# Spreading sixty-four multiply-adds on VectorE over sixteen gate products instead of nine

## The chip, the cores and the metric

One NeuronCore of a Trainium2 chip runs the whole program. The metric is the time of one execution on the device in microseconds (us), taken as the median of several executions; a profiled execution gives the rows quoted here.

## The reference, cut to what matters

The program is a two-layer backbone over 512 latent tokens and 256 context tokens with 2048 features. Layer 0 is an attention mixer, layer 1 a Fourier mixer. For this change, layer 1 matters:

```python
m = silu(cvec) @ ada_w + ada_b            # shift, scale, gate: 3 x 2048
h = layer_norm(x) * (1.0 + scale) + shift
u, gate = split(h @ w_in)                 # 4096 columns each
f = fft2(u in groups of 256).real         # over tokens and group
o = (f * silu(gate)) @ w_out
x = layer_norm(ALPHA * x + g_l * o) * ln_g + ln_b
```

The vector `m` of layer 1 has 6144 values, twelve chunks of 512. The chunks 0 to 7 (shift and scale) are needed before layer 1 starts. The chunks 8 to 11 (the gate `g_l`) are needed only when layer 1's output is scaled, long after the gate products. These four chunks are what the change moves.

## The kernel before, in words

**Where we are.** The Fourier layer runs in `fourier` (L1254 on): `transforms` makes the operands, `gates` computes the gate path in sixteen products g = 0 to 15 and stores silu of each, `mix` computes sixteen products for the other half and multiplies, then two output stages follow. `gates` takes the stretch from about 1218 to 1577 us.

**One gate product.** `product_pair` (L1194 on) forms one [256 x 2048] by [2048 x 512] product from seven smaller ones (i = 0 to 6), by combining 2 x 2 blocks. Each of the seven splits a weight block in two parts (high on ScalarE at L41 into `wh`, low on VectorE at L44 into `wl`), then TensorE multiplies 24 pairs of 128 x 128 by 128 x 256 (L54). The seven use the operands `ba`, `bb`, `bt` (four of them) and `bc`, and then the next gate begins with `ba` again. VectorE also adds block sums for the next product (L1183, L1184, L1185), changes one sum (L1206) and combines results from PSUM (L1212 to L1221, tile `c`). ScalarE applies silu (L1354, tile `sgo`), and its queue stores the result. `wh` and `wl` have three buffers each. So a split can start when the product three places back has ended.

**What is called between the products.** After product i the function `mid(i)` is called. `ahead` (L1228 on) acts at i = 4: it puts four weight loads of 512 KB each (`wraw`) on SyncE's queue and the three block sums for the next gate on VectorE. The weight loads go round five buffers, so they wait for the splits and sums that read the old blocks. In the gates 0 to 7 a further step at i = 6 loads a block of `hf` on SyncE's queue, forms four combinations on GpSimd (L1160 to L1165) and stores them from GpSimd's queue (`ht`).

**The conditioning chunks.** `mac_start` (L229) makes a generator, `tick` (L234) advances it by one step, `mac_rest` (L238) runs what is left. One step (`ada_steps`, L184 on) takes one tile `macraw` of [128, 2, 512] (512 KB), and does two multiply-adds of 128 x 512 on VectorE (L195 for the first of a chunk, L197 for the others) into a tile `mac`; then it issues the load of the next `macraw`. Four chunks of eight steps make 32 steps, 64 multiply-adds and 32 loads. When a chunk is full, the next tick calls `ada_col` (L215 on): four small matmuls of `mac` with a column of ones on TensorE into the PSUM tile `psm` (L219), then a small add on VectorE (L223) into `g1`.

**What sets the order.** From here to the end `pinned` is true, and every matmul stays in program order on TensorE. The loads of SyncE's queue are issued with `late`, so they stay in program order too. The multiply-adds, splits and sums on VectorE aren't held (`mac_hold` is False): the framework chooses their place in VectorE's instruction order at build time, and the engine then works strictly in that order.

**Before the change** `tick` is called at i = 0, 2, 4 and 6 of the gates 0 to 8. That is four steps and eight multiply-adds a gate. The 32 steps end with gate 7 and the last `ada_col` comes in gate 8. The gates 9 to 15 have none. `macraw` and `mac` have three buffers each at the right side of SBUF, freed after gate 8; there the five buffers of `stage` follow, which hold operands for the first product of `mix` (`spread` at L1245 splits them while gate 15 still runs).

Of the kernel before, what the change touches and what calls it, by code (L numbers as in the profile page):

```python
# [10 lines left out]
F32 = mybir.dt.float32  # L11
# [4 lines left out]
PSUM = bass.MemoryType.PSUM  # L16
# [8 lines left out]
class Build:  # L25
# [1314 lines left out]
    def gates(self, f, pair, ops):  # L1340
        nc = self.nc
        st = f.enter_context(ExitStack())
        sp = self.pool(st, "sgp", 1)
        with ExitStack() as m:
            macp = self.pool(m, "mac5", 3, side="right")
            tp = self.pool(m, "tmp5", 3, side="right")
            psm = self.pool(m, "psm5", 1, space=PSUM)
            self.mac_start(macp, lambda: tp.tile([128, 512], F32, name="mac"), lambda: psm.tile([128, 512], F32, name="psm5"),
                           [(1, 8), (1, 9), (1, 10), (1, 11)], 2)

            def gate(g, mid=self.ahead):
                c = pair(ops, mid)
                v = sp.tile([128, 4, 256], F32, name="sgo")
                nc.scalar.activation(out=v, in_=c, func=AF.Silu)  # L1354
                self.nc.scalar.dma_start(out=self.sg_d[g], in_=v)

            for g in range(9):
                def mid(i, g=g):
                    if i % 2 == 0:
                        self.tick()  # L1360
                    self.ahead(i)
                    if g < 8 and i == 6:
                        hf = tp.tile([128, 8, 256], F32, name="hf5", bufs=1)
                        self.load(hf[:, 4:8, :].rearrange("p a b -> p (a b)"), self.hf_d[g].rearrange("p a b -> p (a b)"), True)
                        self.combo_terms(hf[:, 6, :], hf[:, 7, :], hf[:, 4, :], hf[:, 5, :], hf[:, 0:4, :])
                        self.store(self.ht_d[:, :, g, :], hf[:, 0:7, :])
                gate(g, mid)
            self.mac_rest()
        self.fu = f.enter_context(ExitStack())
        self.stage_pool(self.fu, 5, self.ht_d)  # L1370
        for g in range(9, 16):
            gate(g)
            if g == 11:
                self.stage(5)
        st.close()

    def mix(self, f, pair, ops):
# [324 lines left out]
```

## Time and profile before

| | |
|---|---|
| median of 3 runs | 2333.34 us (2333.04 to 2336.59) |
| profiled execution, its own time | 2323.94 us |
| its span, first to last instruction | 2322.2 us |
| mean granted TensorE clock | 0.976 of full speed |
| TensorE matmul busy | 2147.6 us, 92% |
| VectorE busy | 1886.4 us, 81% |
| ScalarE busy | 947.0 us, 41% |
| GpSimd busy | 429.0 us, 18% |

Rows speak of PE (TensorE), DVE (VectorE), ACT (ScalarE), POOL (GpSimd) and SP (SyncE); a "q" behind the name is the engine's queue, which issues transfers. The profiled execution is 9.4 us below the median of the runs, so a saving read from its rows is subtracted from the median.

### The profile page before, as it was taken

The numbers are of one execution on the slowest core, as the hardware profiler recorded it, in microseconds if no ns is written. First come the engines' busy times: TensorE is split into PE (matmuls) and PEld (weight loads), VectorE is DVE, ScalarE is ACT, GpSimd is POOL, SyncE is SP. The second block draws the span as 40 slices with busy tenths as digits, with TensorE's granted clock in tenths as the row PEclk, the third lists the DMA queues.
The fourth block names the chain that finished last, engine by engine and source line by source line (L and its number), as shares of the span: only waits on it lengthen the run. The fifth ranks groups of instructions, "written<-read, shape, count | busy, mean of one in ns | idle before, by whom it ended". The sixth has DMA issues, their size and how long they took to land.

```text
span 2322.2 us, 39267 instructions
## 1 busy us (share of the span) xinstructions
PE 2147.6 (92%) x15708; PEld 1994.3 (86%) x15708; DVE 1886.4 (81%) x2603; ACT 947.0 (41%) x1321; POOL 429.0 (18%) x407
## 2 busy tenths in 40 slices
PE   5999989989999999999788999998999998998994
PEld 3778879889899999777568989998999998998994
DVE  5456799998765588677799998789899899779998
ACT  2222344433444467322463333444343445445331
POOL 1023413100111123000551131002122124002003
PEclk9999999999999999999999999999999999999997
DMA  8852354566511132787427765545455446537333
GB/s 339 310 196 95 124 183 159 188 230 208 208 48 58 60 110 75 229 300 261 169 96 252 273 242 181 182 146 188 156 175 193 150 166 230 174 128 255 117 137 118
DMA packets 128702, 412.63 MB, mean 178 GB/s; under 512 B 14852, under 2 KB 15492, under 8 KB 126728
## 3 DMA queue, kind: packets, MB, share of 16 engines
q1 hardware_dynamic: 113144, 359.04, 45.3%
q0 software_dynamic: 8320, 31.33, 3.8%
q10 hardware_dynamic: 7056, 19.76, 2.2%
q8 instruction: 123, 2.02, 0.4%
q14 instruction: 59, 0.48, 0.1%
HBM read 347.81 MB, written 62.26 MB: 177 GB/s over the span
## 4 chain that ended last, share of the span: by engine, by line
PE 35%; DVE 8%; DMA 3%; issue 3%; ACT 1%; POOL 1%; DVEq 0%; SPq 0%; ACTq 0%; POOLq 0%
PE r L54 33%; DVE wl L44 2%; DMA wraw<-in_wg 2%; PE psd L54 1%; DVE mac L197 1%; DMA stage<-yt 1%; DVE wraw L1185 1%; DVE btl L44 1%; DVE ws L1206 0%; DVE x L1539 0%; DVE c L1219 0%; PE pt L1492 0%; DVE hf L1325 0%; DVE x L1535 0%; POOL btl L44 0%
## 5 line engine op out<-in xcount | busy, mean ns | idle before, releaser
L54 PE MATMUL r<-bth,wl 128*128 128x256 f32 x1848 | 525.1, 284 | 16.8 <-DVE wl L44 16.5
L54 PE MATMUL r<-btl,wh 128*128 128x256 f32 x1848 | 524.6, 284 | 2.3 <-DVE btl L44 1.3
L54 PE MATMUL r<-bth,wh 128*128 128x256 f32 x1848 | 525.2, 284 | 0.2 <-ACT wh L41 0.2
L41 ACT CAST wh<-wraw 128x1024 fp32r<-128x1024 f32 x262 | 274.6, 1050 | 393.1 <-PE r L54 288.0
L44 DVE TENSOR_TENSOR wl<-wraw,wh 128x1024 fp32r<-128x1024 f32 x262 | 335.0, 1283 | 52.3 <-ACT wh L41 52.0
L54 PEld LDWEIGHTS r<-bth,wl 128*128 128x128 f32 x1848 | 351.4, 190 | 19.5 <-DVE wl L44 19.2
L54 PEld LDWEIGHTS r<-btl,wh 128*128 128x128 f32 x1848 | 350.8, 190 | 3.6 <-DVE btl L44 1.7
L54 PEld LDWEIGHTS r<-bth,wh 128*128 128x128 f32 x1848 | 351.8, 190 | 0.9 <-issue 0.5
L41 ACT CAST wh<-ws 128x1024 fp32r<-128x1024 f32 x183 | 191.8, 1049 | 344.3 <-PE r L54 330.4
L44 DVE TENSOR_TENSOR wl<-ws,wh 128x1024 fp32r<-128x1024 f32 x183 | 230.0, 1257 | 12.0 <-ACT wh L41 9.8
L197 DVE SCALAR_TENSOR_TENSOR mac<-macraw,cs,mac 128x512 f32<-128x512 f32 x240 | 193.6, 807 | 11.4 <-DMA macraw<-in_ada 9.9
L54 PE MATMUL r<-hlh,wl 128*128 128x256 f32 (+1 forms) x480 | 147.2, 307 | 26.7 <-DVE wl L44 26.6
L54 PE MATMUL r<-hlh,wh 128*128 128x256 f32 (+1 forms) x480 | 146.3, 305 | 0.6 <-ACT wh L41 0.5
L54 PE MATMUL r<-hll,wh 128*128 128x256 f32 (+1 forms) x480 | 144.9, 302 | 0.0
L54 PE MATMUL r<-bah,wl 128*128 128x256 f32 x384 | 112.7, 293 | 25.1 <-DVE wl L44 25.1
L54 PEld LDWEIGHTS r<-hlh,wl 128*128 128x128 f32 x480 | 93.5, 195 | 33.7 <-DVE wl L44 30.7
L41 ACT CAST pgh<-raw 128x512 fp32r<-128x512 f32 (+2 forms) x104 | 65.7, 662 | 121.8 <-DMA raw<-in_wo 78.2
L54 PE MATMUL r<-bbh,wl 128*128 128x256 f32 x384 | 109.5, 285 | 2.9 <-DVE wl L44 2.9
L54 PE MATMUL r<-bal,wh 128*128 128x256 f32 x384 | 111.2, 290 | 0.0
L54 PE MATMUL oacc<-pgl,yh 128*128 128x512 f32 x256 | 102.1, 399 | 9.7 <-DVE pgl L44 9.7
L54 PE MATMUL r<-bah,wh 128*128 128x256 f32 x384 | 111.1, 289 | 0.0
L54 PE MATMUL r<-bbh,wh 128*128 128x256 f32 x384 | 109.4, 285 | 0.0
(489 smaller groups left out, 5700.1 us busy)
## 6 DMA issues: line engine op xcount, KB each, us to landing
macraw<-in_ada SPq DMA_DIRECT2D x72, 512.0 KB, 6.3
wraw<-in_win SPq DMA_DIRECT2D x66, 512.0 KB, 6.7
raw<-in_adas SPq DMA_DIRECT2D x64, 512.0 KB, 5.1
wraw<-in_wg SPq DMA_DIRECT2D x64, 512.0 KB, 6.6
wraw<-in_wu SPq DMA_DIRECT2D x64, 512.0 KB, 4.3
wraw<-in_wo SPq DMA_DIRECT2D x64, 512.0 KB, 4.7
macraw<-in_ada SPq DMA_DIRECT2D x112, 256.0 KB, 3.9
raw<-in_wo SPq DMA_DIRECT2D x40, 512.0 KB, 5.4
```

Source lines behind the costliest of these rows:

```text
L41: ins = nc.scalar.copy(out=hi, in_=src)
L44: sub = (eng or nc.vector).tensor_sub(out=lo, in0=src, in1=hi.bitcast(F32))
L54: self.pin(self.nc.tensor.matmul(ps, lhsT=a, rhs=b, start=start, stop=stop))
L197: ins = nc.vector.scalar_tensor_tensor(out=acc, in0=raw[:, k, :], scalar=col, in1=acc, op0=ALU.mult, op1=ALU.add)
L1185: nc.vector.tensor_sub(out=raw[1, 0], in0=raw[0, 0], in1=raw[1, 0])
```

## The change

The pools of the conditioning work move out of the inner scope and live through the stage on the left side, with two buffers for `macraw` (three before) and two for `mac` (three before). `hf` alone stays on the right side. `tick` is called at i = 1 and 5 instead of 0, 2, 4, 6, and in all sixteen gates instead of nine. So a gate has two steps and four multiply-adds. `ada_col` falls in the gates 4, 8 and 12 (it was in 2, 4, 6 and 8), and the last one after gate 15, in `mac_rest`.

```diff
         st = f.enter_context(ExitStack())
         sp = self.pool(st, "sgp", 1)
+        macp = self.pool(st, "mac5", 2)
+        mp = self.pool(st, "acc5", 2)
+        psm = self.pool(st, "psm5", 1, space=PSUM)
+        self.mac_start(macp, lambda: mp.tile([128, 512], F32, name="mac"), lambda: psm.tile([128, 512], F32, name="psm5"),
+                       [(1, 8), (1, 9), (1, 10), (1, 11)], 2)
         with ExitStack() as m:
-            macp = self.pool(m, "mac5", 3, side="right")
-            tp = self.pool(m, "tmp5", 3, side="right")
-            psm = self.pool(m, "psm5", 1, space=PSUM)
-            self.mac_start(macp, lambda: tp.tile([128, 512], F32, name="mac"), lambda: psm.tile([128, 512], F32, name="psm5"),
-                           [(1, 8), (1, 9), (1, 10), (1, 11)], 2)
+            tp = self.pool(m, "tmp5", 1, side="right")
...
             for g in range(9):
                 def mid(i, g=g):
-                    if i % 2 == 0:
+                    if i in (1, 5):
                         self.tick()
                     self.ahead(i)
...
                 gate(g, mid)
-            self.mac_rest()
         self.fu = f.enter_context(ExitStack())
         self.stage_pool(self.fu, 5, self.ht_d)
         for g in range(9, 16):
-            gate(g)
+            def mid(i):
+                if i in (1, 5):
+                    self.tick()
+                self.ahead(i)
+            gate(g, mid)
             if g == 11:
                 self.stage(5)
+        self.mac_rest()
         st.close()
```

## Rows read from the trace of the kernel before

**Rows 1.** The page's first part: busy time, share of the span, instructions.
```profile
PE 2147.6 (92%) x15708; PEld 1994.3 (86%) x15708; DVE 1886.4 (81%) x2603; ACT 947.0 (41%) x1321; POOL 429.0 (18%) x407
```

**Rows 2.** Busy time by stretch, one gate each; then PE clock, DMA share, GB/s.
```profile
1217.80:1246.86 29.06, 22.70 (x169) 21.86 (x168) 27.86 (x33) 11.93 (x12) 5.26 (x6) 0.94 0.66 219
1246.86:1270.92 24.06, 21.12 (x172) 20.91 (x173) 22.82 (x28) 8.68 (x9) 6.26 (x6) 0.99 0.75 271
1270.92:1295.17 24.25, 23.07 (x182) 22.87 (x182) 22.09 (x27) 8.68 (x10) 5.58 (x5) 0.94 0.75 259
...
1388.67:1413.01 24.34, 20.47 (x167) 19.85 (x166) 21.92 (x26) 8.68 (x10) 7.29 (x7) 1.00 0.66 238
1413.01:1434.02 21.01, 21.01 (x178) 21.01 (x177) 16.73 (x19) 8.59 (x9) 0.00 (x0) 1.00 0.57 189
1434.02:1454.18 20.16, 20.16 (x170) 20.16 (x169) 15.74 (x17) 8.58 (x10) 0.00 (x0) 1.00 0.39 131
...
1554.98:1576.01 21.03, 21.03 (x178) 21.03 (x177) 19.82 (x21) 15.06 (x17) 1.71 (x1) 1.00 0.45 144
```

**Rows 3.** Waits of PE, from 1215 to 1425 us, then from 1425 to 1640.
```profile
PE r L54 <- DVE wl L44: 21.8, 12, 3.5
...
PE r L54 <- DVE wl L44: 9.5, 4, 4.0
```

**Rows 4.** Groups on DVE, 1246.86 to 1413.01 us (gates 1 to 7).
```profile
L197 DVE SCALAR_TENSOR_TENSOR mac<-macraw,cs,mac 128x512 f32<-128x512 f32 x53 | 44.3, 836 | 0.0
L44 DVE TENSOR_TENSOR wl<-wraw,wh 128x1024 fp32r<-128x1024 f32 x30 | 40.1, 1347 | 0.4 <-ACT wh L41 0.4
...
L1183 DVE TENSOR_TENSOR ws<-wraw 128x1024 f32<-128x1024 f32 x7 | 8.6, 1223 | 9.5 <-DMA wraw<-in_wg 9.5
...
L223 DVE TENSOR_TENSOR g<-psm,adab 128x4 f32<-128x4 f32 x3 | 0.5, 158 | 3.2 <-PE psm L219 3.2
```

**Rows 5.** Groups on DVE, 1434.02 to 1554.98 us (gates 9 to 14).
```profile
L44 DVE TENSOR_TENSOR wl<-wraw,wh 128x1024 fp32r<-128x1024 f32 x24 | 29.4, 1226 | 13.7 <-ACT wh L41 13.7
...
L1221 DVE TENSOR_TENSOR c<-r,c 128x256 f32<-128x256 f32 x6 | 2.5, 425 | 4.2 <-PE r L54 4.2
```

**Rows 6.** Timeline of DVE at the end of gate 1: start, duration, instruction.
```profile
1265.43 1.23 DVE L197 SCALAR_TENSOR_TENSOR mac<-macraw,cs,mac 128x512 f32<-128x512 f32 x1
...
1268.42 1.74 DVE L44 TENSOR_TENSOR wl<-wraw,wh 128x1024 fp32r<-128x1024 f32 x1
```

**Rows 7.** Timeline of PE at the start of gate 2.
```profile
1270.21 0.42 PE L54 MATMUL r<-bah,wl 128*128 128x256 f32 x1 [2.31 <-DVE wl L44]
...
1274.44 0.95 PE L219 MATMUL psm<-ones,mac 128*128 128x1 f32 x8
```

**Rows 8.** SP: its waits in gates 1 to 7, its timeline in gate 1; then the chain.
```profile
SPq L62 <- DVE mac L197: 65.4, 15, 10.7
...
1250.35 4.64 SPq L62 DMA_DIRECT2D wraw<-in_wg  x4
...
1252.91 7.53 DMA wraw<-in_wg
```

**Rows 9.** Timeline of DVE in gate 14, then of PE there.
```profile
1544.81 1.22 DVE L1183 TENSOR_TENSOR ws<-wraw 128x1024 f32<-128x1024 f32 x1
...
1547.41 1.22 DVE L44 TENSOR_TENSOR wl<-ws,wh 128x1024 fp32r<-128x1024 f32 x1
...
1550.02 1.22 DVE L44 TENSOR_TENSOR wl<-wraw,wh 128x1024 fp32r<-128x1024 f32 x1
...
1551.03 0.28 PE L54 MATMUL r<-bch,wh 128*128 128x256 f32 x1
...
1553.91 0.28 PE L54 MATMUL r<-bah,wh 128*128 128x256 f32 x1
```

**Rows 10.** Timeline of DVE from gate 15 into the first product of the mix.
```profile
1558.34 1.23 DVE L44 TENSOR_TENSOR wl<-wraw,wh 128x1024 fp32r<-128x1024 f32 x1 [0.74 <-ACT wh L41]
...
1612.32 1.23 DVE L44 TENSOR_TENSOR wl<-wraw,wh 128x1024 fp32r<-128x1024 f32 x1 [1.81 <-ACT wh L41]
```

## The prediction, made before the changed kernel was run

> **What bounds the kernel now.** I read the page first, then the busy time gate by gate, the waits, the groups of VectorE in the two halves of the stage, the timelines, and the queue of SyncE. Over the span TensorE's matmuls are busy 92% [rows 1], so time can be won only where TensorE stands. The gate table shows where [rows 2]. A row runs from one gate's silu to the next. From gate 9 on a gate takes 20.16 us with TensorE busy through all of it, while VectorE works 15.74 us. The gates 1 to 7 take 166.15 us together (1246.86 to 1413.01), 23.74 a gate, with VectorE busy 21.69 us on the mean of the seven rows (first 22.82, last 21.92). So in the first half VectorE alone needs more than TensorE's 20.16. TensorE's waits there are all for `wl`, the low part of a split weight: 21.8 us in 12 waits, the longest 3.5 [rows 3]. The multiply-adds of the conditioning chunks are VectorE's largest group in this stretch [rows 4]; they are absent from gate 9 on.
>
> One stall shows the mechanism. At the end of gate 1 a multiply-add of step i = 6 runs at 1265.43, the split of gate 2's first weight ends only at 1270.16 [rows 6], and TensorE starts at 1270.21 after 2.31 us of waiting [rows 7]. The matmul behind it took 0.42 us where it takes 0.28 in gate 14 [rows 7, 9], and the mean granted clock of that gate is 0.94 [rows 2]: for a few us the clock is at 1.2 instead of 2.4 GHz. That costs 24.25 x 0.06 = 1.5 us more.
>
> VectorE also stands still in gates 1 to 7: 9.5 us at the block sum L1183 for the landing of a weight, 3.2 us at the small add L223 for TensorE [rows 4]. The weight is late since SyncE's queue is in order: it waited 65.4 us for multiply-adds to free `macraw` buffers. In gate 1 it could issue the four weight loads only from 1250.35; one landed 7.53 us after 1252.91 [rows 8].
>
> **The change, part by part.**
>
> *Price of a multiply-add.* Eight of them and all that disturbs them make 21.69 - 15.74 = 5.95 us of VectorE in a gate: 0.74 each [rows 2]. Four fewer give back 2.98.
>
> *Gates 1 to 7.* VectorE needs 15.74 + 2.98 = 18.7 us, or 19.2 if disturbance by GpSimd, which doesn't go, is priced by itself: the splits of raw blocks take 1347 ns against 1226 from gate 9 on, 30 of them in seven gates, 0.5 us a gate [rows 4, 5]. Both are under 20.16, so TensorE becomes the bound. Lower end: 20.16 a gate. Upper end: VectorE keeps all its idle time of 23.74 - 21.69 = 2.05, so 19.2 + 2.05 = 21.25 a gate. I take the lower end and 3 us of leftover stalls over the seven, since the weights also come earlier (below). One `ada_col` remains here (gate 4) where there were three; gate 8, which had one and nothing else, took 21.01, so it costs 0.85 [rows 2]; the matmuls alone are 0.95 [rows 7]. Sum: 7 x 20.16 + 0.85 + 3 = 145.0. **Gain 21.2** (16.5 to 24.2).
>
> *Gate 0.* It takes 29.06 us with VectorE busy 27.86 [rows 2]. It holds eight multiply-adds; four go, 3.0 us. Its first wait, for the first split after the transforms, stays. **Gain 2.5** (0 to 4).
>
> *Gate 8.* It had no multiply-adds and gets four, but VectorE's 16.73 + 2.98 stays under 20.16, and `ada_col` is in it before and after. **0.**
>
> *Gates 9 to 15.* Four multiply-adds each, 2.98 us, go into VectorE's idle time of 20.16 - 15.74 = 4.42 us. That idle time is waiting for `wh` and for TensorE [rows 5], and lies in the first half of a gate, where the pair of i = 1 falls. The pair of i = 5 falls into the full half. There a split is ready early: in gate 14 the last split ends at 1548.63 and is used at 1551.03, the next gate's first ends at 1551.24 and is used at 1553.91 [rows 9]. The cover is 2.40 us, the pair takes 1.48. If both pairs fell there, 0.6 us a gate would show; nothing can be gained. **Loss 0.5** (0 to 4). `ada_col` in gate 12 adds **0.85**; TensorE, all busy there, can't hide it.
>
> *Into the mix.* From 1558.34 VectorE works with hardly a break until 1610.5 (the wait of 1.81 us before 1612.32) [rows 10], since the splits of `stage` join in. TensorE has its 9.5 us of waits of the second half here [rows 3]. What gate 15's four multiply-adds (2.98 us) can't put into gaps like the 0.74 us before 1558.34 moves everything behind them: **loss 2.0** (0.7 to 3.0). The last `ada_col`, 0.85, stands before mix's first product, partly where TensorE waits anyhow: **loss 0.4** (0 to 0.85).
>
> *The queues.* SyncE still issues 32 loads of 512 KB, now one ahead of each gate's four weight loads and one behind them, where three stood ahead and one behind. With two buffers the load for step n + 1 waits for the multiply-adds of step n - 1. The one ahead of the weights waits for those of i = 5 of the gate before; in gate 1 the last pair ran before gate 2's first matmul [rows 6, 7], so the weights are released near a gate's start, earlier than now. Behind it wait the weights, then L1183 and the splits; I price no delay, and its failure is a rival. The `hf` load and GpSimd's work stay behind the gate's last `macraw` load as before. `macraw` and `mac` stand at the left from gate 0 on, and `stage` takes the place of `hf` at the right; no wait comes of that, as far as I see. The DMA share in gate 9 is 0.39 [rows 2], so sixteen more loads find room. On GpSimd's and ScalarE's queues nothing is added. At the start the first `macraw` load comes one product later; nothing but the first pair waits for it. These go at zero.
>
> *Sum.* 21.2 + 2.5 - 0.5 - 0.85 - 2.0 - 0.4 = 19.95, say **20 us**. The profiled execution has 2323.94 us, so it would be 2304; the median of the runs is 9.4 us higher, and the forecast is 2333.34 - 20 = **2313**.
>
> *A rule against it.* GpSimd's combinations keep running in the gates 0 to 7, and VectorE's instructions are longer beside them: a multiply-add took 1.23 us and a split 1.74 [rows 6], against means of 0.84 and 1.35 [rows 4]. Over a gate the splits show the 0.5 us found above. The Trainium skill, SBUF — State Buffer, section "Who interferes with whom", says that a VectorE instruction with two SBUF inputs and a GpSimd instruction that reads SBUF hold the shared port in turn, and that the later one is blocked wholly. By that alone the sum would be about zero in gates 1 to 7; it is the second rival. The trace disagrees in the amount.
>
> **The rivals.**
>
> 1. *The stall follows the multiply-adds, not VectorE's fullness.* The gates 1 to 7 lose 23.74 - 20.16 - 3 x 0.85 / 7 = 3.2 us with eight, so 0.4 us each. Four in every gate then cost 1.6. Gates 1 to 7 gain 166.15 - 141.1 - 11.2 - 0.85 = 13.0, gate 0 gains 1.6, gate 8 loses 1.6, the gates 9 to 15 lose 11.2 + 0.85, the mix 2.4: a loss of 1.5, **2335**. For it: VectorE's order is chosen by the framework. Against it: 4.42 us idle and 2.40 us of cover [rows 2, 9].
>
> 2. *GpSimd blocks VectorE wholly.* GpSimd is busy 5.58 us in gate 2 [rows 2]. Then VectorE needs 18.7 + 5.6 = 24.3 us, as long as a gate takes now, and gates 1 to 7 gain nothing: 2.5 - 0.5 - 0.85 - 2.0 - 0.4 = a loss of 1.25, **2335**. Against it: with eight multiply-adds it would be 27.3, and a gate took 23.74.
>
> 3. *The ring of two holds back the weights* (the slower side). The block sum L1183 runs at 1544.81, 11.1 us after gate 14's first matmul (1553.91 - 20.16) [rows 9]. With a landing of 7.53 us [rows 8] its loads must be out some 3 us into a gate. If the i = 5 pair of the gate before ends later than that, L1183 blocks VectorE's order, and the 0.9 us of cover left after the pair is gone. With 1 us of stall and 1.5 of lowered clock a gate takes 22.7: gates 1 to 7 gain 166.15 - 158.6 - 0.85 = 6.7, gate 8 loses 2.5, the gates 9 to 15 lose 17.5 + 0.85, the mix 2.4: a loss of 16.6, **2350**. For it: SyncE's 65.4 us of such waits [rows 8]. Against it: in gate 1 the i = 6 pair was over before 1268.42, about when gate 2 could have begun (1270.21 - 2.31), some 3 us ahead of that point, with twice the multiply-adds in front of it.
>
> **How the numbers follow.** The forecast has 0.86, rival 1 0.05, rival 2 0.03, rival 3 0.06. Best case of the terms: 24.2 + 4 - 0.85 - 0.7 = 26.6, 2307; worst: 16.5 - 4 - 0.85 - 3.0 - 0.85 = 7.8, 2326. VectorE's order elsewhere may shift by a few us too, so I give 2304 to 2326; under 2 in 10 are left out, the rivals and the tails. A measurement of this kernel can tell 0.2%, 4.7 us, from no change. Faster 0.86 (the forecast), same 0.08 (rivals 1 and 2), slower 0.06.
>
> **What would show it.** Right: gates 1 to 7 near 20.2 to 21 us with VectorE near 19, clock 1.00, TensorE's waits for `wl` from 21.8 down to a few us, no wait of L1183 for a weight; gates 9 to 14 still 20.16 with VectorE near 18.7 (gate 12 21.0); the mix starting with some 2 us more VectorE work. Wrong: waits of a few us per gate in the second half (rival 1), GpSimd's combinations with long VectorE instructions beside them and gates near 24 us (rival 2), L1183 waiting for weights behind `macraw` loads in all gates (rival 3).

## The result, and the profile after

The changed kernel took 2304.53 us (median of 4, 2301.56 to 2308.92), the kernel before, run beside it on the same chip, 2333.19 us. The ratio is 0.9884 (95% interval 0.9868 to 0.9900), so the change saves 1.2%, 23 to 31 us. The forecast was 2313 us, a saving of 20, with a range of 2304 to 2326. The measured time is 8.5 us below the forecast and half a us inside the fast end of the range.

The two profiled executions differ by less: 2323.94 and 2301.56 us, 22.4 us. The reason lies ahead of the stage. Up to the first gate matmul both programs have the same instructions in the same order on every engine, but this matmul comes at 1217.42 us before and at 1221.96 after. In the fourteen profiled executions of this study it lies between 1217.4 and 1228.0. So a stretch is compared from its own first instruction, not from the start of the program. From the first gate matmul to the first result of the mix (`yt`) it is 397.84 us before and 371.00 after: 26.8 us. Behind that the two agree to 0.1 us (706.90 and 706.83).

| stretch (us) | before | after | gain | forecast |
|---|---|---|---|---|
| first matmul to silu of gate 0 | 29.44 | 27.20 | 2.2 | 2.5 |
| gates 1 to 7 | 166.15 | 142.22 | 23.9 | 21.2 |
| gate 8 | 21.01 | 19.44 | 1.6 | 0 |
| gates 9 to 15 | 141.99 | 142.01 | 0.0 | -1.35 |
| silu of gate 15 to the first `yt` | 39.25 | 40.13 | -0.9 | -2.4 |
| sum | 397.84 | 371.00 | 26.8 | 20.0 |

The busy time by gate of the changed kernel answers to [rows 2], in the same columns: bounds and length, then PE, PEld, DVE, ACT, POOL, clock, DMA share, GB/s. Its first row begins with the first gate matmul.

```profile
1221.96:1249.16 27.20, 24.52 (x190) 24.28 (x189) 27.07 (x33) 12.04 (x12) 4.46 (x4) 0.94 0.72 231
1249.16:1268.19 19.03, 19.03 (x161) 19.03 (x160) 18.93 (x22) 8.58 (x10) 7.37 (x6) 1.00 0.79 272
1268.19:1290.35 22.16, 22.16 (x187) 22.16 (x186) 20.82 (x23) 8.68 (x10) 7.29 (x8) 1.00 0.70 238
...
1370.39:1391.38 20.99, 20.99 (x177) 20.99 (x177) 19.20 (x22) 8.68 (x9) 7.03 (x7) 1.00 0.71 250
...
1410.82:1430.98 20.16, 20.16 (x170) 20.16 (x169) 18.02 (x22) 8.59 (x11) 0.00 (x0) 1.00 0.55 183
...
1471.30:1492.35 21.05, 21.05 (x178) 21.05 (x177) 18.28 (x23) 8.58 (x10) 0.00 (x0) 1.00 0.57 197
```

From gate 1 on PE's busy column equals the length of every stretch, and the clock is 1.00. Single gates of the first half are longer or shorter than 20.16 since silu starts earlier or later behind the last product. TensorE's own first matmuls of the gates 1 and 8 show what that hides:

```profile
1246.67 0.29 PE L54 MATMUL r<-bah,wh 128*128 128x256 f32 x1
...
1388.68 0.29 PE L54 MATMUL r<-bah,wh 128*128 128x256 f32 x1
```

They are 142.01 us apart, which is 7 x 20.16 and one `ada_col` of 0.89: no stall is left. Before, the same two are 163.8 us apart (1244.39 to 1408.15). So a stretch from silu to silu can differ by some 2 us from TensorE's own, and differences of that size between single stretches say nothing. Gate 12 shows its `ada_col`, 21.05.

The waits of PE from 1200 to 1425 us, then from 1535 to 1640, answer to [rows 3]:

```profile
PE r L54 <- DVE wl L44: 2.7, 1, 2.7
...
PE r L54 <- DVE btl L44: 5.7, 3, 2.7
PE r L54 <- DVE wl L44: 3.8, 1, 3.8
PE r L54 <- POOL btl L44: 0.9, 1, 0.9
```

One wait of 2.7 us is left of 21.8: that for the very first split. Into the mix PE waits 10.4 us where it waited 9.5.

The groups on DVE in the gates 1 to 7 (1249.16 to 1391.38) answer to [rows 4]:

```profile
L44 DVE TENSOR_TENSOR wl<-wraw,wh 128x1024 fp32r<-128x1024 f32 x28 | 38.1, 1371 | 0.2 <-ACT wh L41 0.2
L197 DVE SCALAR_TENSOR_TENSOR mac<-macraw,cs,mac 128x512 f32<-128x512 f32 x28 | 25.5, 912 | 0.0
...
L1183 DVE TENSOR_TENSOR ws<-wraw 128x1024 f32<-128x1024 f32 x7 | 8.6, 1224 | 1.9 <-DMA wraw<-in_wg 1.7
```

SP's waits for multiply-adds in the same stretch answer to the first of [rows 8]:

```profile
SPq L62 <- DVE mac L197: 1.4, 1, 1.4
```

VectorE's busy time in these gates falls from 151.81 us to 135.61, 19.4 a gate:

```profile
1249.16:1391.38 142.22, 142.22 (x1188) 142.22 (x1187) 135.61 (x150) 60.59 (x63) 43.26 (x38) 1.00 0.74 254
```

There are half as many multiply-adds, but their mean is longer than before (912 ns against 836): a larger part of those left lies beside GpSimd's work. And two things vanished together: SP's waits for multiply-adds (65.4 to 1.4 us) and L1183's wait for a weight (9.5 to 1.7). The timeline of DVE at the end of gate 2 shows the first split of gate 3 (1284.02) ahead of the pair, where [rows 6] had it behind:

```profile
1282.88 1.22 DVE L1184 TENSOR_TENSOR ws<-ws,wraw 128x1024 f32<-128x1024 f32 x1
1284.02 1.78 DVE L44 TENSOR_TENSOR wl<-wraw,wh 128x1024 fp32r<-128x1024 f32 x1
1285.72 0.68 DVE L1219 TENSOR_TENSOR c<-c,r 128x512 f32<-128x512 f32 x1
1286.32 1.32 DVE L197 SCALAR_TENSOR_TENSOR mac<-macraw,cs,mac 128x512 f32<-128x512 f32 x1
```

So three things changed at once: VectorE's work in a gate, the time at which weights come, and the order that the framework chose on VectorE. The prediction's sum prices only the first. The experiments take them apart as far as they can.

### The profile page after: what moved, and what is told of

Its sections match the earlier page's. It is cut to its first block, busy times and chain, and to the rows that moved or that the text cites. A ratio compares the mean times of both kernels' runs of the same rounds, so it can differ in the third digit from the quotient of the medians.

```text
span 2299.8 us, 39256 instructions
## 1 busy us (share of the span) xinstructions
PE 2136.4 (93%) x15708; PEld 1986.7 (86%) x15708; DVE 1883.0 (82%) x2603; ACT 947.4 (41%) x1321; POOL 429.7 (19%) x407
## 5 line engine op out<-in xcount | busy, mean ns | idle before, releaser
L54 PE MATMUL r<-bbl,wh 128*128 128x256 f32 x384 | 109.6, 285 | 0.0
```

What stands on the lines that cost most here:

```text
L54: self.pin(self.nc.tensor.matmul(ps, lhsT=a, rhs=b, start=start, stop=stop))
```

## The experiments

The measure is the time of the gates 1 to 7, silu to silu, in the profiled execution: 166.15 us before, 142.22 after. The ratio is that of the whole kernel to the one before, run beside it. Three `ada_col` lie in these gates in the kernel before and in e1, e2, e5, e9, e10, e12 and e14, one in the changed kernel and in e3, e7, e8 and e13, none in e6. So 1.7 of the change's 23.9 us here are two `ada_col` that moved to later places.

| run | multiply-adds, loads a gate | gates 1 to 7 | first matmul to `yt` | ratio (interval) |
|---|---|---|---|---|
| before | 8, 4 | 166.15 | 397.84 | 1 |
| changed | 4, 2 | 142.22 | 371.00 | 0.9884 (0.9868 to 0.9900) |
| e1 loads first | 8, 4 | 167.15 | 397.49 | 0.9990 (0.9976 to 1.0003) |
| e2 half the adds | 4, 4 | 155.17 | 381.69 | 0.9931 (0.9910 to 0.9953) |
| e3 adds twice | 8, 2 | 154.74 | 391.67 | 0.9963 (0.9948 to 0.9978) |
| e5 rings of two | 8, 4 | 160.55 | 387.22 | 0.9961 (0.9938 to 0.9983) |
| e6 no steps | 0, 0 | 139.72 | 367.03 | 0.9866 (0.9843 to 0.9888) |
| e7 gates 1 to 14 | 4 or 6, 2 or 3 | 143.47 | 371.06 | 0.9877 (0.9855 to 0.9899) |
| e8 two steps, rings of three | 4, 2 | 142.57 | 371.19 | 0.9885 (0.9860 to 0.9909) |
| e9 large steps | 8, 2 of 1 MB | 151.78 | 383.03 | 0.9923 (0.9897 to 0.9950) |
| e10 sums later | 8, 4 | 151.70 | 380.58 | 0.9929 (0.9905 to 0.9953) |
| e12 half, sums later | 4, 4 | 156.28 | 384.27 | 0.9919 (0.9898 to 0.9941) |
| e13 twice, no combinations | 8, 2 | 144.09 | 382.61 | 0.9931 (0.9906 to 0.9956) |
| e14 half, two hf buffers | 4, 4 | 155.69 | 384.71 | 0.9933 (0.9910 to 0.9956) |

**Work against loads: e2 and e3.** The first leaves out the second multiply-add of every step in the kernel before. The second does every one twice in the changed kernel.

```diff
 # e2
             for k in range(nk):
+                if self.some and k % 2:
+                    continue
 # e3
                     self.tc.keep_in_program_order(ins)
+                if self.some:
+                    nc.vector.scalar_tensor_tensor(out=acc, in0=raw[:, k, :], scalar=col, in1=acc,
+                                                   op0=ALU.mult, op1=ALU.add)
```

> The kernel before with the second of the two multiply-adds of every step left out, so half of each conditioning sum is missing; loads, rings and places of the steps stay as before. Four multiply-adds a gate, as in the changed kernel, but in the gates 0 to 8 alone. Theory (VectorE's work a gate): the gates 1 to 7 take 142 to 148 us (166.2 before), nearly all of the gain, though SyncE's order is the old one. Rival (SyncE's order and the weights): three conditioning loads still stand ahead of the weights, so the gates 1 to 7 stay above 155 us.

> The changed kernel with every multiply-add of this stage done twice on the same data (the sums come out other than the reference's), without one load more: eight a gate, in all sixteen gates. Theory (a threshold on VectorE): the gates 1 to 7 go back to 21.7 us or more each (152 to 166 us together, 142.2 in the changed kernel), and in the gates 9 to 14, where VectorE needs 15.74 + 8 x 0.67 = 21.1 us at least, a gate takes 21.1 to 23 us instead of 20.16; the kernel is 20 to 45 us slower than the changed one. Rival (the gates 0 to 8 were slow through GpSimd's combinations, hf loads or late weights): the gates 9 to 14 stay at 20.16. Rival (a price for each multiply-add rather than a threshold): the changed kernel's gates would have to show half of this one's loss, and they show none.

Leaving out half of the multiply-adds gives 11.0 us of the 23.9. My range for e2, 142 to 148, was missed, and the rival's bound of 155 was just met. Doubling them in the changed kernel loses 12.5 in these gates, as expected; the whole kernel loses some 18 us by the two ratios, a little under the expected 20. The four cells of the table (166.2, 155.2, 154.7, 142.2) add up almost exactly: 11.0 to 12.5 us for the multiply-adds, 11.4 to 13.0 for what came with thinner loads (1.7 of it the two `ada_col`). My theory had given nearly all to the work.

But neither run changes the work alone: in both, the framework also chose another order of the splits and sums on VectorE. It shows in where TensorE waits. Before, 17.0 of its 17.8 us of waits in the gates 1 to 7 stand at a gate's first product (`ba`, as in [rows 7]); in e2, 6.7 of 8.2 stand at its last (`bc`), for instance:

```profile
1309.32 0.39 PE L54 MATMUL r<-bch,wl 128*128 128x256 f32 x1 [1.66 <-DVE wl L44]
```

What VectorE itself waits for in e2, in the gates 1 to 7, is one thing (L1185 there is L1183 before; the edit moved the lines by two):

```profile
DVE ws L1185 <- DMA wraw<-in_wg: 16.2, 5, 3.7
DVE ws L1185 <- issue: 7.1, 2, 3.7
```

23.3 us of waiting for weights, with VectorE otherwise free: it is busy 131.5 of 155.2 us. In e3 the gates 9 to 14 hold a surprise, in the columns of [rows 2]:

```profile
1423.49:1546.37 122.88, 122.88 (x1019) 122.37 (x1018) 121.79 (x152) 51.52 (x55) 0.00 (x0) 1.00 0.58 203
```

Eight multiply-adds a gate take 20.33 to 20.36 us, `ada_col` aside (gate 12, 21.17), with VectorE full and GpSimd at 0.00. I had expected 21.1 us at least, from single durations; behind one another they take less room (a split recorded with 1.22 us is followed by the next instruction after 1.13). So eight fit into TensorE's 20.16 but for 0.2 us.

**GpSimd's part: e13.** The same doubling without the combinations in the gates 0 to 7.

```diff
-                        self.combo_terms(hf[:, 6, :], hf[:, 7, :], hf[:, 4, :], hf[:, 5, :], hf[:, 0:4, :])
-                        self.store(self.ht_d[:, :, g, :], hf[:, 0:7, :])
+                        self.store(self.ht_d[:, 0:4, g, :], hf[:, 4:8, :])
+                        self.store(self.ht_d[:, 4:7, g, :], hf[:, 4:7, :])
```

> The run with every multiply-add twice, without GpSimd's combinations in the gates 0 to 7 (the hf block is stored in their place, so the output is not the reference's; the transfers keep their size, in two stores). Theory (with eight multiply-adds a gate takes 20.35 us where GpSimd is idle, gates 9 to 14, and 22.1 where it combines, so GpSimd's share is some 1.7 us a gate): the gates 1 to 7 take 142 to 147 us (154.7 with the combinations). Rival (late loads and the order on VectorE make the difference): 151 us or more.

The gates 1 to 7 fall from 154.74 to 144.09, most of them to 20.33 to 20.36 us, as in the second half. VectorE has the same instructions in the same order as in e3; they are shorter (a split of a raw block takes 1216 ns where e3 has 1360), and it is busy 141.70 us where it was 150.13. So with eight multiply-adds GpSimd's four combinations cost 1.5 us a gate, and they alone make the first half's gates longer than the second's:

```profile
1252.61:1396.70 144.09, 142.69 (x1179) 141.77 (x1179) 141.70 (x177) 60.18 (x63) 10.68 (x14) 1.00 0.75 249
```

**Who makes the weights late: e1, e14, e9.** In e1 all four steps are called behind the weight loads.

```diff
-                    if i % 2 == 0:
-                        self.tick()
                     self.ahead(i)
+                    for _ in range((0, 0, 0, 0, 1, 1, 2)[i]):
+                        self.tick()
```

> The kernel before with its four steps a gate in the gates 0 to 8, but all four called behind the weight loads of i = 4 (one at i = 4, one at 5, two at 6). So the weights go out ahead of the conditioning loads, and VectorE's work a gate stays at eight multiply-adds. Theory (VectorE has more to do in a gate than TensorE): the waits of L1183 for a weight go (9.5 us in the gates 1 to 7), but VectorE still needs 21.7 us a gate, so the gates 1 to 7 take 152 to 162 us (166.2 before, 142.2 after) and the kernel wins 4 to 14 us, at most half of the change's 28. Rival (the late weights behind SyncE's waits were the cause): the gates 1 to 7 fall to 142 to 147 us and the kernel wins 20 us or more.

Neither came out: 167.15, no gain at all. The waits of VectorE in the gates 1 to 7 point to why: L1183 waits 3.5 us where it waited 9.5, but now the multiply-adds wait for their own data, in front of splits.

```profile
DVE mac L197 <- DMA macraw<-in_ada: 8.7, 5, 4.6
DVE ws L1183 <- DMA wraw<-in_wg: 3.5, 3, 1.6
```

In this run something is late on VectorE either way. (e10 below has four loads too and waits for none, so it isn't their number alone.) In e2's queue the longest wait was that of the `hf` load for the store of `ht`, so e14 gives `hf` a second buffer in e2; order and instructions stay the same on every engine.

```diff
-            tp = self.pool(m, "tmp5", 3, side="right")
+            tp = self.pool(m, "tmp5", 2, side="right")
...
-                        hf = tp.tile([128, 8, 256], F32, name="hf5", bufs=1)
+                        hf = tp.tile([128, 8, 256], F32, name="hf5", bufs=2)
```

> The run with half of the multiply-adds (the second of every step left out, four conditioning loads a gate), with two buffers for the hf block instead of one (and two for mac instead of three, so that it fits). Every engine has the same instructions in the same order as in that run. There L1183 waited 23 us for weights, and SyncE's queue waited 30 us for the store of ht before it could load the next hf, with the conditioning loads and the weights behind. Theory A (the hf load's wait is what makes the weights late): that wait goes, L1183's wait falls under 8 us, and the gates 1 to 7 take 142 to 149 us (155.2 there, 142.2 in the changed kernel). Theory B (the conditioning loads' waits for multiply-adds do it, 44 us on SyncE's queue): the waits move to them, and the gates 1 to 7 stay at 152 us or more.

SP's waits in the gates 1 to 7, first in e2, then in e14:

```profile
SPq L62 <- DMA ht<-hf: 30.4, 7, 6.1
...
SPq L62 <- DMA macraw<-in_ada: 9.4, 6, 2.6
```

```profile
SPq L62 <- DMA macraw<-in_ada: 32.2, 6, 7.2
```

Theory A falls, theory B stands: the wait for `ht` went, but L1185 still waits 20.7 us, and the gates stay at 155.69. The conditioning loads took the wait over: for the landing of earlier `macraw` loads and for multiply-adds they wait 65.3 us together, where it was 44.3 in e2. The same bytes in two loads of 1 MB instead of four of 512 KB are e9:

```diff
-            macp = self.pool(m, "mac5", 3, side="right")
+            macp = self.pool(m, "mac5", 2, side="right")
...
-                           [(1, 8), (1, 9), (1, 10), (1, 11)], 2)
+                           [(1, 8), (1, 9), (1, 10), (1, 11)], 4)
...
-                    if i % 2 == 0:
+                    if i in (1, 5):
                         self.tick()
```

> The kernel before with steps of four multiply-adds and loads of 1 MB, two a gate at i = 1 and 5, in the gates 0 to 8: eight multiply-adds and the same bytes a gate as before, but two conditioning loads instead of four, and rings of two. Theory: VectorE's work (151.8 us in the gates 1 to 7) stays the floor; with one load ahead of the weights instead of three the rest goes, so the gates 1 to 7 take 151 to 157 us. Rival (the bytes, not the number of loads, make the weights late): 160 us or more.

151.78, as the theory said, and VectorE waits 1.2 us for weights; the DMA share is 0.79, higher than the 0.73 of the kernel before over its gates 1 to 7. So bytes and bandwidth alone don't make the weights late. What is left is their place: how many conditioning loads, each tied to a multiply-add that must first free its buffer, stand ahead of the weights in SyncE's queue. That is argued from the waits and not shown by itself, since e9 also changes the places of the steps, the ring and VectorE's order.

**VectorE's order: e10 and e12.** The block sums of the gates 0 to 8 are called at i = 6, the weight loads stay at i = 4. e12 is e10 with half of the multiply-adds.

```diff
-                    self.ahead(i)
+                    if i == 4:
+                        src = self.todo.pop(0)
+                        self.later = self.block_loads(src)
+                    elif i == 6:
+                        self.nxt.append(self.blocks(None, self.later))
```

> The kernel before with the block sums of the gates 0 to 8 called at i = 6 instead of i = 4; the weight loads stay at i = 4, and the eight multiply-adds and four conditioning loads a gate stay as they were. So a late weight holds up VectorE's order three splits later, and the next gate's first split no longer stands behind the three sums and a pair of multiply-adds. Theory as it stands after the first four runs (two causes of about 11 to 13 us each in the gates 1 to 7: VectorE's work a gate, and the weights that come late behind SyncE's queue): the wait of L1183 goes, the work stays, and the gates 1 to 7 take 151 to 158 us (166.2 before, 154.7 in the run with eight multiply-adds and the new order). Rival (work a gate alone, the first theory): 163 us or more. Rival (order alone): under 146 us.

> Both repairs on the kernel before, without its loads thinned or its rings changed: the block sums called at i = 6, and the second multiply-add of every step left out (half of each conditioning sum is missing). Theory (the two causes add up: VectorE's work a gate, and late weights that hold up its order): the gates 1 to 7 take 140 to 144 us, as in the changed kernel (142.2), with four conditioning loads a gate still on SyncE's queue. Rival (the four loads themselves cost something, by bandwidth or by the queue): 147 us or more.

e10 is the cleanest of all, in the columns of [rows 2]:

```profile
1251.08:1402.78 151.70, 148.58 (x1215) 147.36 (x1216) 151.27 (x179) 60.82 (x64) 44.41 (x36) 0.99 0.77 279
```

Eight multiply-adds, four loads, and VectorE busy 151.27 of 151.70 us: nothing but work. In the stage it has the instructions of the kernel before, in the same order on every engine and queue but VectorE. There, in gate 1, the next gate's first split (1268.47) now comes ahead of two sums and the pair:

```profile
1267.34 1.22 DVE L1183 TENSOR_TENSOR ws<-wraw 128x1024 f32<-128x1024 f32 x1
1268.47 1.22 DVE L44 TENSOR_TENSOR wl<-wraw,wh 128x1024 fp32r<-128x1024 f32 x1
1269.60 1.76 DVE L1184 TENSOR_TENSOR ws<-ws,wraw 128x1024 f32<-128x1024 f32 x1
```

In the kernel before VectorE was busy 151.81 of 166.15, and the 14.3 us between were mostly the 9.5 at L1183 and the 3.2 at L223 of [rows 4]. SyncE's queue still waits 47.3 us for multiply-adds in e10, but no sum waits for a weight any more. So of the 23.9 us, 14.4 were VectorE's order and the late weights that held it up, which this run doesn't separate. The remaining 9.5 are the distance from VectorE's work to the changed kernel's 142.22, with the 1.7 of the two `ada_col` in it. e10 is the kernel before with one call moved, and it wins 0.7%.

e12 missed: 156.28. With half of the multiply-adds the framework put the sums just where they had been (two other instructions of the stage moved on VectorE), and L1183 (there L1185) waited 23.3 us as in e2:

```profile
DVE ws L1185 <- DMA wraw<-in_wg: 20.9, 6, 4.7
DVE ws L1185 <- issue: 2.4, 1, 2.4
```

The edit didn't make the order it was meant to make, so this run says nothing on whether the two repairs add up.

**The rings: e5 and e8.** The smaller rings alone on the kernel before, and the thinner steps alone with rings of three (its steps end with gate 8, incomplete).

```diff
 # e5
-            macp = self.pool(m, "mac5", 3, side="right")
-            tp = self.pool(m, "tmp5", 3, side="right")
+            macp = self.pool(m, "mac5", 2, side="right")
+            tp = self.pool(m, "tmp5", 2, side="right")
 # e8
-                    if i % 2 == 0:
+                    if i in (1, 5):
                         self.tick()
...
-            self.mac_rest()
```

> The kernel before with rings of two for macraw and mac instead of three, and nothing else: the change's smaller rings alone. Theory: a smaller ring only ties SyncE closer to VectorE; where VectorE is the bound it makes the weights later still, so the gates 1 to 7 take 166 to 180 us (166.2 before) and the kernel is 0 to 14 us slower. Rival (the smaller rings or their new place give the gain): the kernel wins 10 us or more.

> The kernel before with its rings of three at the right side, but two steps a gate at i = 1 and 5 in the gates 0 to 8, as the changed kernel has them; the steps that don't fit into nine gates are left out (14 of 32, so two of the four chunks stay zero or unfinished). This is the thinning alone, without the smaller rings and the new place in memory. Theory: the gates 1 to 7 take 141 to 146 us (142.2 in the changed kernel), so the rings of two neither help nor hurt. Rival (the rings of two are part of the gain, as the run with the rings alone suggests): 148 us or more.

e5 went the other way than I expected: the smaller rings make the kernel before faster, 160.55. Its order on VectorE is another one: in gate 4 the next gate's first split comes before two of the sums and the last pair.

```profile
1338.39 1.22 DVE L44 TENSOR_TENSOR wl<-wraw,wh 128x1024 fp32r<-128x1024 f32 x1
1339.53 1.22 DVE L1184 TENSOR_TENSOR ws<-ws,wraw 128x1024 f32<-128x1024 f32 x1
1340.66 1.22 DVE L1185 TENSOR_TENSOR wraw<-wraw 128x1024 f32<-128x1024 f32 x1
1342.40 0.75 DVE L197 SCALAR_TENSOR_TENSOR mac<-macraw,cs,mac 128x512 f32<-128x512 f32 x1
```

With two steps a gate the ring does nothing: e8 gives 142.57 with rings of three against 142.22 with rings of two. So the smaller rings are no part of the gain. That they make room for the steps beside `stage` in the second half is their likely use; no run shows it.

**What is left: e6 and e7.** No steps in this stage (their chunks set to zero), and steps in the gates 1 to 14 only.

```diff
 # e6, in both halves of the stage
-                    if i in (1, 5):
-                        self.tick()
 # e7
-                    if i in (1, 5):
+                    if g and i in (1, 5):
                         self.tick()
...
-            def mid(i):
-                if i in (1, 5):
+            def mid(i, g=g):
+                if g < 15 and i in ((1, 3, 5) if g in (9, 10, 11, 13, 14) else (1, 5)):
```

> The changed kernel without any conditioning step in this stage (four of the twelve chunks of layer 1 are set to zero). What is left of the cost of the steps in the changed kernel: four ada_col of 0.85 us, some 2 us in gate 0, some 1 to 2 us into the mix. Theory: the stretch from the first gate matmul to the mix's first result is 3 to 8 us shorter than in the changed kernel (371.0 us there), gates 1 to 7 near 141.1 us. Rival (the multiply-adds still cost something in every gate): 10 us or more.

> The changed kernel with the steps in the gates 1 to 14 only: two a gate in 1 to 8 and 12, three in 9, 10, 11, 13 and 14, all chunks complete, the last ada_col inside gate 14. Theory: gate 0 and the start of the mix lose their multiply-adds, where VectorE is full, and gates 9 to 14 have room for six (15.74 + 6 x 0.67 = 19.8 of 20.16): the stretch from the first gate matmul to the mix's first result gets 1 to 4 us shorter than in the changed kernel (371.0), the kernel 0 to 4 us faster, which rounds can hardly tell. Rival (a third step a gate stalls TensorE in 9 to 14): those gates rise above 20.16 and the stretch gets longer.

Without any steps the stretch is 4.0 us shorter than in the changed kernel, and four `ada_col` of 0.85 us are 3.4 of that: the 64 multiply-adds are hidden but for half a us. (Its 139.72 for the gates 1 to 7 is the effect of silu's place again: TensorE's own time there is 141.12, 7 x 20.16.) e7 missed its 1 to 4 us: it ends at the same 371.06. The third step a gate costs little: 123.99 us in the gates 9 to 14 are 120.96 and three `ada_col` and 0.5. From silu of gate 15 to `yt` it takes 1.8 us less, 0.9 of it because that silu starts later, but the last `ada_col` is now in a gate where TensorE is full. Its ratio can't be told from the changed kernel's.

## Why the prediction was right, point by point

**TensorE stands for VectorE's splits, and the change ends that.** Right. The waits for `wl` fall from 21.8 to 2.7 us (the prediction puts the 21.8 into the gates 1 to 7, but 4.0 of it lie in gate 0), the clock is 1.00 from gate 1 on, the gates 9 to 14 stay at 20.16 with VectorE near 18.0, gate 12 at 21.05.

**Gates 1 to 7.** Gain 23.9 against 21.2, inside the bounds (16.5 to 24.2), at their good end. The mis-sized term is the 3 us of leftover stalls: none is left. VectorE's need came out at 19.4 us a gate, close to the 18.7 and 19.2 of the sum; GpSimd's share in it was taken too small (0.5 us a gate from the splits of raw blocks, 1.5 with eight multiply-adds in e13), but below 20.16 that costs nothing.

The weak step is the one behind it: VectorE's need is under 20.16, "so TensorE becomes the bound", and at worst VectorE keeps the idle time of 2.05 us a gate that it had. e2 shows that this doesn't follow. There VectorE is busy 18.8 us a gate, idle 3.4, and a gate takes 22.2, above the prediction's upper end of 21.25; the gain of 11.0 is below its lower bound of 16.5. In the changed kernel the step held because VectorE's waits went too. The prediction has this in half a sentence, that the weights also come earlier. The half sentence is right (SP's waits for multiply-adds fall from 65.4 to 1.4 us, L1183's from 9.5 to 1.7), but order and late weights together were 14.4 of the 23.9 us (e10), without a term of their own, and the work was 9.5 (e10) to 12.5 (e3). That the framework would put the first split ahead of the pair was not foreseen at all. So the path was right, and part of the size was luck.

**Gate 0.** 2.2 against 2.5.

**Gate 8.** 1.6 against 0, and this is silu's place, not a saving of its own. TensorE's wait of 3.5 us, the longest of [rows 3], ends at 1412.03, ahead of gate 7's silu at 1413.01, so the row of gate 8 never held it. Counted from TensorE's first matmul of gate 1 to that of gate 9, it is 188.56 us before and 163.06 after: 25.5, the sum of the two rows. The 163.06 are 8 x 20.16 and two `ada_col`.

**Gates 9 to 15 and into the mix.** These belong together, since silu of gate 15 starts 0.9 us sooner behind its product and only moves the border between the two rows. Together 0.9 us were lost where 3.75 were forecast, and gate 12's `ada_col` (0.89) alone is as much. The idle time of VectorE took the multiply-adds, as forecast; e7 shows room for six. The 2.0 us for gate 15's multiply-adds in front of the mix were too much. The changed program has another order of the `stage` splits on VectorE and ScalarE here, so the term isn't a plain shift; I didn't trace it further.

**The rivals.** A price for each multiply-add (rival 1) is excluded by the changed kernel, whose gates take TensorE's own time with four of them in both halves, and by e6, where leaving all 64 out gives half a us. Rival 3 (the rings of two hold back the weights) is excluded by L1183's 1.7 us of waits over seven gates, and by e8: two and three are alike. Rival 2 asked for GpSimd to block VectorE for all its 5.6 us a gate; e13 shows 1.5. The Trainium skill, SBUF — State Buffer, section "Who interferes with whom", says that a VectorE instruction with two SBUF inputs contends with a GpSimd instruction that reads SBUF. This case agrees that the two collide: a multiply-add takes 912 ns on the mean in the changed kernel's first half against 746 in e3's second half, where GpSimd is idle, and taking GpSimd's combinations out gives the time back (e13). Priced by all of GpSimd's busy time, as rival 2 did, the collision would have cost more than was measured; how much of that time falls beside such instructions was not measured.

**The whole.** The terms' best case was a gain of 26.6 us, or 2307. The stretch gave 26.8, and the medians differ by 28.7. So the measured 2304.53 is inside the range only through the 3 us added for VectorE's order elsewhere, and not because of it: that is luck. The saving was rightly taken from the median: the profiled executions before and after differ by 4.5 us ahead of the stage for no reason in the program. Taken from the profiled execution it would have come nearer the measured time, by chance.

## What to carry to other kernels

In this kernel VectorE, which works in order, lost time in three ways that look alike in a wait for its results: too much work, a neighbour that slows it, and one instruction at its head that waits for a transfer. Its busy time against the length of the stretch tells the first from the last (151.8 of 166.2 us before, 151.3 of 151.7 in e10), and each wants another repair. That an engine's work fits into a stretch doesn't yet make another engine the bound: in e2 it fitted and the gate still took 22.2 us. Background work that is spread thinly also thins its loads, so count what stands ahead of the urgent loads in an in-order queue; and look at the built order of an engine after every edit, since a changed ring (e5) reordered it and a moved call (e12) hardly did. A border that another engine sets, like silu here, can move by 2 us; check a stretch against the bounding engine's own first instructions.

## What the runs showed of the hardware that I had not expected

The same instructions in the same order ahead of the stage (e6 and e8 have one small zeroing more) reached its first matmul at 1217.4 to 1228.0 us, a spread of over 10 us, as much as several of the edits at issue moved; between the profiled kernels before and after most of it arose from 380 to 590 us, in small steps. GpSimd's four small combinations of 128 x 256 elements (1.4 us each on the mean in e3) cost VectorE 1.5 us a gate where it was full; with four multiply-adds, where it has room, they cost the gates next to nothing (142.22 us for gates 1 to 7 with them, 142.01 for gates 9 to 15 without).
